# The low parts of the weights made on VectorE instead of GpSimd, from the latent attention's value projection on

## The chip, the cores and the metric

The kernel runs on one core of one Trainium2 chip. The metric is the device time of one execution in microseconds (us). Three runs of the kernel before took 795.70 to 796.46 us, median 796.04. Engines are named as in the profile: PE is TensorE (PEld its weight loads), DVE is VectorE, ACT is ScalarE, POOL is GpSimd, SP is the engine that issues most DMAs. L203 is line 203 of the kernel.

## The reference, cut to what matters

One decoder layer on 512 tokens of width 1024: a convolution branch and a latent attention (MLA) branch, merged by gates, then cross attention to 256 memory tokens, then a squared-ReLU MLP and a final norm. All in float32.

```python
u = rms_norm(h, norm_mix_g)
proj = u @ w_in                     # conv input, c_q, c_kv, k_rope, gate logits
conv_out = conformer_conv(...)      # 31 taps, layer norm, silu, @ w_conv_out
mla_out = mla_attention(...)        # q from w_uq, k and v from w_ukv, 8 heads, @ w_mla_out
merged = gates0 * conv_out + gates1 * mla_out
h = h + merged @ w_out
u = rms_norm(h, norm_xattn_g); mem_n = rms_norm(mem, norm_mem_g)
h = h + memory_cross_attention(u, mem_n, w_xq, w_xkv, w_xo)   # 4 heads of 128
u = rms_norm(h, norm_mlp_g)
h = h + square(relu(u @ w_mlp1)) @ w_mlp2
y = rms_norm(h, final_norm_g)
```

## The kernel before, in words

Every matrix product is made of three passes over rounded operands (`mm3`, L231 to L240): each operand is split into a high part, the value cast to the matmul's format, and a low part, the value less its high part; the three products high x high, low x high and high x low are added in PSUM (L237, L238, L239). The high part is a cast on ACT, the low part one subtraction on DVE or POOL (`split`, L201 to L203; `split_scaled` at L206 and L207 is the same with a factor).

Activations are split once, on ACT and DVE. Weights arrive in raw chunks by DMA from SP (tile `raw`, two buffers, L315) and are split piece by piece just before their use by `prep` (L324): a piece is mostly 128x1024, its high part `wh` and low part `wl` have three buffers each. Which engine makes `wl` is held in a variable, `w_eng[0]`: DVE for the second convolution channel tile, POOL from the third on (L638), DVE again from the cross attention's output projection on (L1147).

A small pipe (`Pipe`) issues the split of the next piece before the matmuls of the piece in hand. PE runs in the order in which the program is written; the order on the other engines is set by a scheduler that goes by estimates of its own, so the place of an instruction on DVE or ACT can differ from its place in the program. Each engine then works through its queue strictly in that order.

The stretch that matters here runs from the value projection to the end of the cross attention's scores. In program order:

- heads: k and v (`k_pair` and the loop that fills `vh`, `vl`), q per head (`q_head`, product with the rotary table into `qtmp` at L763, then split into `q`), `scores` (row maximum `m` at L794, exp on ACT, scaling of `p` at L800), `transp` (transposes of `p` on PE at L810, split into `pt`), `pv` (split into `oh`, `ol`). The convolution's output projection `conv_out` lies between (`gates` at L828). In every odd step of the loop a piece of `uq` (128x768) and one of `co` (128x1024) are split.
- output projection of the attention and merge: `evac_mla` takes each of 8 columns from PSUM times its gate (`mt`, L916), adds the convolution's part (L917) and splits the sum into `mgh` on ACT and `mgl` on DVE.
- `out_unit`: 8 units of 24 matmuls over all 8 merged columns, then `Norm.add` (residual `ht` at L976, its split `hgl` at L207, sum of squares at L983). Memory tokens are normalised meanwhile (`mem_norm`, with `mh` on ACT and `ml` on DVE).
- memory keys `xk_unit` (`xkt`, `xkl`), and beside it the inverse root of the norm (`rsqrt`, L245 to L250, tiny DVE instructions in a chain), whose result PE broadcasts by four transposes (L271).
- cross attention: queries `xq_unit` (`xt`, `xql`), `xscores`, `xtransp`, values `xv_unit`, `xpv`.

The MLP behind it has POOL issue DMAs only.

Of the kernel before, what the change touches and what calls it, by code (L numbers as in the profile page):

```python
# [168 lines left out]
def _body(tc, a):  # L169
# [3 lines left out]
    dve = nc.vector  # L173
# [27 lines left out]
    def split(hi, lo, src, eng=None):  # L201
        act.copy(hi, src)  # L202
        (eng or dve).tensor_tensor(lo, src, hi.bitcast(F32), op=ALU.subtract)  # L203
# [94 lines left out]
    def chunk_hbm(i):  # L298
        n = stream[i][3] * len(stream[i][4])
        return a["weights"][offs[i]:offs[i] + P * n].rearrange("(p n) -> p n", p=P)  # L300

    def raw(*key):
        ci = ch[key]
        while issued[0] < n_ring and issued[0] < ci + RAW_BUFS:
            i = issued[0]
            _, _, _, kt, cols = stream[i]
            n = kt * len(cols)
            t = wp.tile([P, 2048], F32, tag="raw", name="raw", bufs=RAW_BUFS)
            src = chunk_hbm(i)
            raws[i] = t[:, :n].rearrange("p (k m) -> p k m", k=kt)  # L310
            if i == 1:
                for sl in (slice(0, 128), slice(128, 256)):
                    dma(out=raws[i][:, :, sl], in_=src.rearrange("p (k m) -> p k m", k=kt)[:, :, sl])
            else:
                dma(out=t[:, :n], in_=src)  # L315
            issued[0] += 1
        return raws[ci]

    def whl(kt, cols):
        hi = wp.tile([P, 1024], F32R, tag="wh", name="wh", bufs=3)  # L320
        lo = wp.tile([P, 1024], F32R, tag="wl", name="wl", bufs=3)
        return tuple(t[:, :kt * cols].rearrange("p (k m) -> p k m", k=kt) for t in (hi, lo))

    def prep(key, k0=0, kt=None, c0=0, cols=128):  # L324

        r = raw(*key)
        kt = r.shape[1] if kt is None else kt
        hi, lo = whl(kt, cols)
        split(hi, lo, r[:, k0:k0 + kt, c0:c0 + cols], w_eng[0])
        return hi, lo  # L330

    w_eng = [dve]
# [233 lines left out]
    def proj_unit(key, c0, evac):  # L566
        def main(hl):
            b = bank()
            mm3(b, [(lhs(hl, k), (uh[:, k, :], ul[:, k, :])) for k in range(KD)])
            evac(b)  # L570
        pipe.unit(lambda: prep(key, c0=c0), main)
# [147 lines left out]
    def evac_gate(b, i):  # L719
        t = wkp.tile([P, S], F32, tag="sg", name="sg")  # L720
        dve.tensor_tensor(t, b, rbx, op=ALU.mult)  # L721
        act.activation(gates[:, i, :], t, AF.Sigmoid)
# [4 lines left out]
    for i in range(16):  # L727
# [2 lines left out]
                c_unit("ckv", j, KVL + ROPE, c_tags, ckv_done)  # L730
        proj_unit(("gate", i // 2), 128 * (i % 2), lambda b, i=i: evac_gate(b, i))
    split(wkk[:, 0], wkk[:, 1], raw("wk"))
    hlv = prep(("wv",), cols=512)
    pipe.flush()
    while not taps[1]:
# [408 lines left out]
                        n2.add(m, bs[m])  # L1144
        pipe.unit(lambda: prep(("xo", m2 // 2), c0=256 * (m2 % 2), cols=256), main)

    w_eng[0] = dve  # L1147
    for m2 in range(4):
        xo_unit(m2)
    pipe.ahead(lambda: prep(("m1", 0)))  # L1150
# [387 lines left out]
```

## Time and profile before

| | us |
|---|---|
| median of three runs | 796.04 |
| the profiled execution | 797.19 |
| its span, first to last instruction | 795.4 |
| PE busy (3594 matmuls) | 761.3 (96%) |
| DVE busy | 535.3 (67%) |
| ACT busy | 400.6 (50%) |
| POOL busy | 169.7 (21%) |
| mean granted clock of TensorE | 0.984 |

Busy time is the time in which at least one instruction of the engine ran; matmuls overlap, so a matmul of 390 ns on 128x512 starts about 227 ns after the one before. Of POOL's busy time 144.6 us are its 65 low parts at L203; of the chain that ended last PE holds 70% and DVE 19%. The granted clock is the share of full speed that TensorE was given: 1.00 is 2.4 GHz, 0.50 is 1.2 GHz.

### The profile page before, as it was taken

Reading aid. Unit: us, or ns where it says so; the run is one execution under the profiler, and the core shown is the slowest. Engines: PE = TensorE matmul, PEld = TensorE weight load, DVE = VectorE, ACT = ScalarE, POOL = GpSimd, SP = SyncE. Lnnn points to the kernel's source line nnn. Section 1 sums busy time; section 2 is a strip of 40 time slices with the busy share of each in tenths; the row PEclk is TensorE's granted clock in tenths of the full one; section 3 lists DMA queues with packets and bytes.
Section 4 is the critical chain, followed back from the end, with each engine's and each line's share of the span. In section 5 each row is a group of like instructions: output and inputs, shape, how many; then the busy total and the mean of one; then the engine's idle time right before and its main releaser. Section 6 shows DMA issues by size and latency. Waiting matters only on the chain.

```text
span 795.4 us, 9520 instructions
## 1 busy us (share of the span) xinstructions
PE 761.3 (96%) x3594; PEld 627.8 (79%) x3594; DVE 535.3 (67%) x812; ACT 400.6 (50%) x681; POOL 169.7 (21%) x103
## 2 busy tenths in 40 slices
PE   8799999999999998998999999999999979999996
PEld 4589788778788886788887888888888858888785
DVE  5798999843888859758686833243333446667995
ACT  7323333469666537343465644444343445655562
POOL 4444336423312215346320000000000000111000
PEclk9899999999999999899999999999999998999998
DMA  8213223222102144124132324425353596999731
GB/s 280 97 40 113 76 84 128 84 90 97 54 0 107 54 157 162 58 102 146 68 105 106 118 108 146 171 82 224 106 188 129 165 283 239 227 236 213 198 106 53
DMA packets 26989, 103.36 MB, mean 130 GB/s; under 512 B 2368, under 2 KB 9920, under 8 KB 17984
## 3 DMA queue, kind: packets, MB, share of 16 engines
q1 hardware_dynamic: 13600, 67.54, 23.8%
q0 software_dynamic: 2304, 16.78, 10.4%
q10 hardware_dynamic: 11040, 18.45, 6.7%
q8 instruction: 28, 0.46, 0.2%
q14 instruction: 17, 0.14, 0.1%
HBM read 94.37 MB, written 8.39 MB: 129 GB/s over the span
## 4 chain that ended last, share of the span: by engine, by line
PE 70%; DVE 19%; DMA 4%; ACT 4%; issue 3%; SPq 0%; DVEq 0%; ACTq 0%
PE mm L239 18%; PE mm L237 18%; PE mm L238 18%; DVE cv L494 6%; PE at L238 4%; PE at L239 4%; PE at L237 4%; DMA a<-weights 2%; DVE q L203 1%; DVE mt L917 1%; DMA x<-weights 1%; DVE rs_t L248 1%; DMA xr<-xT 1%; PE at L810 1%; DVE sg L721 1%
## 5 line engine op out<-in xcount | busy, mean ns | idle before, releaser
L203 POOL TENSOR_TENSOR wl<-raw,wh 128x1024 fp32r<-128x1024 f32 (+4 forms) x65 | 144.6, 2227 | 252.4 <-ACT wh L202 249.3
L202 ACT CAST wh<-raw 128x1024 fp32r<-128x1024 f32 (+4 forms) x103 | 102.6, 998 | 190.0 <-PE mm L238 146.6
L203 DVE TENSOR_TENSOR wl<-raw,wh 128x1024 fp32r<-128x1024 f32 x38 | 46.5, 1224 | 99.6 <-ACT wh L202 99.6
L237 PE MATMUL mm<-hgh,wh 128*128 128x512 f32 x288 | 113.2, 393 | 0.0
L238 PE MATMUL mm<-hgl,wh 128*128 128x512 f32 x288 | 112.2, 390 | 0.0
L239 PE MATMUL mm<-hgh,wl 128*128 128x512 f32 x288 | 112.2, 390 | 0.0
L494 DVE SCALAR_TENSOR_TENSOR cv<-zpad,vec,cv 128x512 f32<-128x512 f32 x116 | 80.2, 752 | 0.1
L1356 POOL DMA_DIRECT2D x<-weights x12 | 10.6, 880 | 293.8 <-DVE wl L203 273.8
L237 PE MATMUL mm<-uh,wh 128*128 128x512 f32 x176 | 70.7, 402 | 2.3 <-DVE sg L721 2.1
L239 PE MATMUL mm<-uh,wl 128*128 128x512 f32 x176 | 69.3, 394 | 0.5 <-DVE wl L203 0.5
L238 PE MATMUL mm<-ul,wh 128*128 128x512 f32 x176 | 69.3, 394 | 0.0
L239 PEld LDWEIGHTS mm<-hgh,wl 128*128 128x128 f32 x288 | 54.1, 188 | 11.4
L237 PEld LDWEIGHTS mm<-hgh,wh 128*128 128x128 f32 x288 | 54.1, 188 | 10.9
L238 PEld LDWEIGHTS mm<-hgl,wh 128*128 128x128 f32 x288 | 54.1, 188 | 10.9
L203 DVE TENSOR_TENSOR wl<-x,wh 128x1024 fp32r<-128x1024 f32 x25 | 30.4, 1223 | 18.9 <-ACT wh L202 18.9
L237 PEld LDWEIGHTS mm<-uh,wh 128*128 128x128 f32 x176 | 33.5, 190 | 10.7 <-issue 4.2
L239 PEld LDWEIGHTS mm<-uh,wl 128*128 128x128 f32 x176 | 33.5, 190 | 8.1 <-DVE wl L203 1.0
L238 PEld LDWEIGHTS mm<-ul,wh 128*128 128x128 f32 x176 | 33.5, 190 | 6.5
L202 ACT CAST wh<-x 128x1024 fp32r<-128x1024 f32 x25 | 26.1, 1048 | 24.4 <-PE at L239 9.7
L238 PE MATMUL at<-wl,hA 128*128 128x512 f32 x96 | 37.6, 392 | 0.6 <-DVE wl L203 0.6
L239 PE MATMUL at<-wh,hB 128*128 128x512 f32 x96 | 37.4, 390 | 0.0
L237 PE MATMUL at<-wh,hA 128*128 128x512 f32 x96 | 37.4, 389 | 0.0
(392 smaller groups left out, 1772.4 us busy)
## 6 DMA issues: line engine op xcount, KB each, us to landing
raw<-weights SPq DMA_DIRECT2D x42, 1024.0 KB, 4.8
x<-weights POOLq DMA_DIRECT2D x12, 1024.0 KB, 11.4
a<-weights SPq DMA_DIRECT2D x5, 1024.0 KB, 8.3
x<-weights SPq DMA_DIRECT2D x4, 1024.0 KB, 5.9
raw<-weights SPq DMA_DIRECT2D x4, 768.0 KB, 4.3
xr<-xT SPq DMA_DIRECT2D x8, 256.0 KB, 6.0
raw<-weights SPq DMA_DIRECT2D x4, 512.0 KB, 5.0
ht<-xT ACTq DMA_DIRECT2D x1, 2048.0 KB, 9.4
```

The source lines that it names most:

```text
L202: act.copy(hi, src)
L203: (eng or dve).tensor_tensor(lo, src, hi.bitcast(F32), op=ALU.subtract)
L237: pe.matmul(out, wh, ah, start=first and i == 0, stop=False, **kw)
L238: pe.matmul(out, wh, al, start=False, stop=False, **kw)
L239: pe.matmul(out, wl, ah, start=False, stop=last and i == n - 1, **kw)
L248: dve.scalar_tensor_tensor(t, dst, -0.5, dst, op0=ALU.mult, op1=ALU.mult)
L494: dve.scalar_tensor_tensor(run if w < CW - 1 else acc[:, c, :], zs, wcol, run, op0=ALU.mult, op1=ALU.add)
L721: dve.tensor_tensor(t, b, rbx, op=ALU.mult)
L810: pe.transpose(b[:, (t - k) * P:(t - k + 1) * P], ptok[h, t][:, k * P:(k + 1) * P], ident)
L917: dve.tensor_tensor(t, t, gates[:, m, :], op=ALU.add)
L1356: gps.dma_start(out=t, in_=hbm(what, c), accum_op=ALU.add, max_dma_last_dim=8192)
```

## The change

`w_eng[0] = dve` moves up: it stood ahead of the cross attention's output projection (`xo_unit`) and now stands ahead of the split of `wv`, the value projection of the latent attention. 33 low parts change engine: 29 of 128x1024 and 4 of 128x768. Lines behind the new place have numbers higher by 2 (by 1 behind the old place).

```diff
@@ -730,6 +730,8 @@
                 c_unit("ckv", j, KVL + ROPE, c_tags, ckv_done)
         proj_unit(("gate", i // 2), 128 * (i % 2), lambda b, i=i: evac_gate(b, i))
     split(wkk[:, 0], wkk[:, 1], raw("wk"))
+
+    w_eng[0] = dve
     hlv = prep(("wv",), cols=512)
     pipe.flush()
     while not taps[1]:
@@ -1144,7 +1146,6 @@
                         n2.add(m, bs[m])
         pipe.unit(lambda: prep(("xo", m2 // 2), c0=256 * (m2 % 2), cols=256), main)
 
-    w_eng[0] = dve
     for m2 in range(4):
         xo_unit(m2)
     pipe.ahead(lambda: prep(("m1", 0)))
```

The order on PE and SP stays as it was. On DVE the scheduler puts the low parts between the other instructions, and some of these change places. Three places follow.

DVE in the output projection, merged columns 6 and 7 and what follows, before:

```order
L916 TENSOR_TENSOR mt_2964<-mm,gates 128x512
L916 TENSOR_TENSOR mt_2982<-mm,gates 128x512
L917 TENSOR_TENSOR mt_2964<-mt_2964,gates 128x512
L917 TENSOR_TENSOR mt_2982<-mt_2982,gates 128x512
L246 TENSOR_SCALAR rm<-rs_i 128x2
L207 SCALAR_TENSOR_TENSOR ml<-mr,vec,mh 128x256
L203 TENSOR_TENSOR mgl<-mt_2964,mgh 128x512
L203 TENSOR_TENSOR mgl<-mt_2982,mgh 128x512
```

And DVE at the same place now:

```order
L918 TENSOR_TENSOR mt_2964<-mm,gates 128x512
L918 TENSOR_TENSOR mt_2982<-mm,gates 128x512
L919 TENSOR_TENSOR mt_2964<-mt_2964,gates 128x512
L919 TENSOR_TENSOR mt_2982<-mt_2982,gates 128x512
L203 TENSOR_TENSOR wl<-raw,wh 128x1024
L203 TENSOR_TENSOR mgl<-mt_2964,mgh 128x512
L203 TENSOR_TENSOR mgl<-mt_2982,mgh 128x512
L203 TENSOR_TENSOR wl<-raw,wh 128x1024
L978 TENSOR_TENSOR ht<-ht,mm 128x512
```

One low part of the weights stands ahead of the last two `mgl`, one behind them; the memory's small instructions have moved behind. The pairs of columns 2, 3 and 4, 5 have one low part each ahead of their `mgl` in the same way.

DVE in an odd step of the heads, from the scaling of `p` to the first `pt` (the transposed probabilities' low part), before:

```order
L799 RECIPROCAL rl<-l 128x1
L800 TENSOR_SCALAR p<-p,rl 128x512
L763 TENSOR_TENSOR qtmp<-mm,tq 128x512
L203 TENSOR_TENSOR q<-qtmp,q 128x512
L203 TENSOR_TENSOR ol<-mm,oh 64x512
L203 TENSOR_TENSOR pt_1990<-at,pt_1990 128x512
```

And DVE at the same place now:

```order
L765 TENSOR_TENSOR qtmp<-mm,tq 128x512
L801 RECIPROCAL rl<-l 128x1
L802 TENSOR_SCALAR p<-p,rl 128x512
L203 TENSOR_TENSOR wl<-raw,wh 128x1024
L203 TENSOR_TENSOR q<-qtmp,q 128x512
L203 TENSOR_TENSOR ol<-mm,oh 64x512
L203 TENSOR_TENSOR pt_1990<-at,pt_1990 128x512
```

A low part of 128x1024 stands ahead of `q`, and `qtmp` ahead of the last scaling. In the first two odd steps another low part, 128x768, stands ahead of the four row maxima.

DVE at the inverse root of the norm ahead of the cross attention, from its first pass on, before:

```order
L248 SCALAR_TENSOR_TENSOR rs_t<-rr 128x4
L958 TENSOR_TENSOR xkt<-mm,rbm 128x256
L249 TENSOR_TENSOR rs_t<-rs_t,rv 128x4
L250 SCALAR_TENSOR_TENSOR rr<-rs_t,rr 128x4
L248 SCALAR_TENSOR_TENSOR rs_t<-rr 128x4
L249 TENSOR_TENSOR rs_t<-rs_t,rv 128x4
L250 SCALAR_TENSOR_TENSOR rr<-rs_t,rr 128x4
L248 SCALAR_TENSOR_TENSOR rs_t<-rr 128x4
L203 TENSOR_TENSOR xkl<-xkt,xkh 128x256
L249 TENSOR_TENSOR rs_t<-rs_t,rv 128x4
L250 SCALAR_TENSOR_TENSOR rr<-rs_t,rr 128x4
```

And DVE at the same place now, from the second pass on:

```order
L248 SCALAR_TENSOR_TENSOR rs_t<-rr 128x4
L203 TENSOR_TENSOR wl<-raw,wh 128x1024
L249 TENSOR_TENSOR rs_t<-rs_t,rv 128x4
L203 TENSOR_TENSOR xkl<-xkt,xkh 128x256
L250 SCALAR_TENSOR_TENSOR rr<-rs_t,rr 128x4
L248 SCALAR_TENSOR_TENSOR rs_t<-rr 128x4
L249 TENSOR_TENSOR rs_t<-rs_t,rv 128x4
L960 TENSOR_TENSOR xkt<-mm,rbm 128x256
L250 SCALAR_TENSOR_TENSOR rr<-rs_t,rr 128x4
```

One low part stands inside the chain, and one `xkt` more.

## Rows read from the trace of the kernel before

**Rows 1.** A stretch: length, busy us of PE, PEld, DVE, ACT, POOL, clock, DMA share, GB/s.

```profile
180.50:424.00 243.50, 233.82 (x1214) 194.35 (x1214) 183.85 (x320) 138.67 (x280) 78.56 (x33) 0.99 0.27 95
```

**Rows 2.** Waits of PE, 180 to 430 us: total, times, longest.

```profile
PE mm L237 <- ACT mgh L202: 3.1, 1, 3.1
PE at L271 <- DVE rr L250: 2.3, 1, 2.3
PE at L789 <- DVE pt L203: 1.5, 3, 0.5
PE at L792 <- DVE q L203: 1.5, 1, 1.5
PE mm L238 <- DVE mgl L203: 0.7, 2, 0.5
PE at L1100 <- DVE xpt L203: 0.5, 1, 0.5
```

**Rows 3.** Groups by form: busy us, mean ns, idle before; low parts on both engines.

```profile
L203 POOL TENSOR_TENSOR wl<-raw,wh 128x1024 fp32r<-128x1024 f32 x49 | 119.3, 2437 | 185.0 <-ACT wh L202 181.9 <-PE at L810 3.1
...
L203 DVE TENSOR_TENSOR wl<-raw,wh 128x1024 fp32r<-128x1024 f32 x38 | 46.5, 1224 | 99.6 <-ACT wh L202 99.6
```

**Rows 4.** One tile's instructions, xql: duration ns min/median/max, first and last start.

```profile
L203 DVE TENSOR_TENSOR xql<-xt,xqh x4: 2459/2470/2486, 383.5 to 402.7; 128x512 fp32r<-128x512 f32 x4
```

**Rows 5.** Time order, DVE and POOL, output projection: start us, us (start to end).

```profile
297.87 1.29 DVE L917 TENSOR_TENSOR mt<-mt,gates 128x512 f32<-128x512 f32 x2
...
301.65 4.96 DVE L917 TENSOR_TENSOR mt<-mt,gates 128x512 f32<-128x512 f32 x2
...
309.10 2.75 DVE L917 TENSOR_TENSOR mt<-mt,gates 128x512 f32<-128x512 f32 x2
...
300.84 5.22 POOL L203 TENSOR_TENSOR wl<-raw,wh 128x1024 fp32r<-128x1024 f32 x2 [20.12 <-ACT wh L202]
```

**Rows 6.** Time order, PE, first unit of the output projection.

```profile
309.30 0.40 PE L237 MATMUL mm<-mgh,wh 128*128 128x512 f32 x1
...
312.10 0.40 PE L237 MATMUL mm<-mgh,wh 128*128 128x512 f32 x1
...
322.93 0.41 PE L239 MATMUL mm<-mgh,wl 128*128 128x512 f32 x1
```

**Rows 7.** Stretches of the output projection and of the cross queries, with granted clock.

```profile
317.47:322.50 5.03, 4.80 (x11) 3.42 (x11) 3.97 (x11) 2.35 (x4) 0.72 (x1) 0.50 0.00 0
...
360.00:385.00 25.00, 22.72 (x152) 20.61 (x151) 17.62 (x26) 10.17 (x14) 14.51 (x6) 1.00 0.36 127
```

**Rows 8.** Time order, DVE, inverse root ahead of the cross attention.

```profile
372.06 2.25 DVE L250 SCALAR_TENSOR_TENSOR rr<-rs_t,rr 128x4 f32<-128x4 f32 x1
...
374.55 0.16 DVE L249 TENSOR_TENSOR rs_t<-rs_t,rv 128x4 f32<-128x4 f32 x1
374.75 2.34 DVE L250 SCALAR_TENSOR_TENSOR rr<-rs_t,rr 128x4 f32<-128x4 f32 x1
```

**Rows 9.** Time order, DVE, an odd step of the heads.

```profile
221.12 0.49 DVE L800 TENSOR_SCALAR p<-p,rl 128x512 f32<-128x512 f32 x1
...
223.15 2.47 DVE L203 TENSOR_TENSOR q<-qtmp,q 128x512 fp32r<-128x512 f32 x1 [0.95 <-ACT q L202]
```

**Rows 10.** Time order, PE: first scores, an odd step of the heads, the broadcast.

```profile
203.89 0.33 PE L792 MATMUL at<-k,q 128*128 128x128 f32 x1 [1.47 <-DVE q L203]
...
222.31 1.28 PE L810 MATMUL at<-kon,p 128*128 128x128 f32 x10
...
226.87 0.33 PE L789 MATMUL at<-k,q 128*128 128x128 f32 x1 [0.51 <-DVE pt L203]
...
377.94 0.65 PE L271 MATMUL at<-kon,rr 128*128 128x128 f32 x4 [2.28 <-DVE rr L250]
```

**Rows 11.** Time order, ACT: casts of the weights ahead of two of the places.

```profile
199.77 1.06 ACT L202 CAST wh<-raw 128x1024 fp32r<-128x1024 f32 x1
...
299.71 2.00 ACT L202 CAST wh<-raw 128x1024 fp32r<-128x1024 f32 x2
```

## The prediction

> **What bounds the kernel now.** The changed instructions all lie between 180 and 424 us, so the first view is the table by stretches: in these 243.5 us PE is busy 233.8, DVE 183.9 and POOL 78.6 [rows 1]. PE is the bound, and only its 9.7 us of idle time, with what follows from it, can be won; DVE is next. The second view, who waited for whom on PE in this stretch, splits the idle time into six releasers, 9.6 us together [rows 2]. None is POOL: all are ACT or DVE. So why should taking work from POOL matter? The third view, groups by form, has one 128x1024 low part at 2437 ns on POOL and 1224 ns on DVE [rows 3]. The fourth, one tile's instructions, has DVE's 128x512 low part of the cross queries (xql) at 2470 ns median [rows 4], while two DVE additions of the same size take 1.29 us together while POOL is idle, which it is for 20 us until 300.84 [rows 5]. In the time order such stretched instructions start while a POOL low part runs: the next two pairs of additions take 4.96 and 2.75 us. I read this as a hold: DVE stands until POOL's instruction is over, at some 1.8 us each (2.47 less 0.65).
>
> **What the change moves.** 33 low parts go from POOL to DVE: 29 of 128x1024 and 4 of 128x768. DVE gets 29 x 1.22 + 4 x 0.92 (three quarters of 1.22) = 39 us; POOL has no arithmetic left in the stretch. Were each of the 33 to hold one DVE instruction now, DVE would get back 33 x 1.8 = 59 us; bounds for DVE's own work are thus -20 and +39 us. What counts is only where PE waits, place by place. PE, SP and the DMA order are the same in both; a raw buffer can come free up to 1 us later or earlier, which I cost at nothing since the casts of the next weights on ACT wait mostly for PE. If that cover is gone, a late cast costs what it is late.
>
> Place 1, output projection. PE starts its first unit at 309.30 and goes on at 0.233 us a matmul (twelve to 312.10) [rows 6]. In before it waits 0.5 us, then 3.07 us for the seventh merged column, and after that the granted clock is 0.50, the 1.2 GHz level, over 317.47 to 322.50 [rows 7]; the thirtieth matmul starts at 322.93. Without any wait it would start at 309.30 + 29 x 0.233 = 316.06, so 6.9 us are lost. Now DVE in the new order, with 0.6 us from start to start for every free 128x512 instruction and 1.22 for a low part: the two additions that start at 301.65 end at 302.9 instead of 306.5 [rows 5]; low part (its high part is cast by 301.7 [rows 11]) to 304.1; two mgl to 305.35; two products to 306.6; two additions to 307.8; low part to 309.0, 0.8 us before PE wants it; two mgl to 310.4 (five casts of the memory stand ahead of their high halves on ACT, which I estimate costs nothing, since DVE is at the low part meanwhile); two products to 311.65; two additions to 312.9; low part to 314.1; the last two mgl at 314.75 and 315.35. PE wants the first of these with its twentieth matmul, 309.30 + 19 x 0.233 = 313.73, and waits 1.05 us. The wait of 2.28 us elsewhere in the stretch [rows 2] was followed by no slow matmuls (granted clock 1.00 over 360 to 385 us [rows 7]), so I let the clock stay at 2.4 GHz. Gain 6.9 - 1.05 = 5.8. Bounds: 6.9 if DVE is 1 us earlier, 0.5 if the wait again reaches 3 us.
>
> Place 2, norm ahead of the cross attention. Two tiny steps of the inverse root take 2.25 and 2.34 us [rows 8], held like the others; free ones start 0.2 us apart. PE stands 2.28 us for them and goes on at 377.94 [rows 10]. In the new order one low part (1.22) and one more xkl (0.4) lie inside the chain instead: 2 x 2.1 less 1.6 is 2.6, more than the wait. Gain 2.3; if the low part first waits for its cast, 1.1.
>
> Place 3, heads. In each of the three odd steps q's low half starts after its cast and is held (2.47 us from 223.15 [rows 9]), the probabilities' low parts follow, and PE waits 0.5 us for a bank at 226.87 [rows 10]. With the weights' low part (1.22) ahead of q instead of a 1.8 us hold inside it, the bank comes about 1 us sooner. Gain 3 x 0.5 = 1.5. A 0.92 us low part ahead of three row maxima is new there; the last scaled row ends at 221.61 and PE's transposes start at 222.31 [rows 9, 10], so 0.7 us cover it, and a held scaling of p goes too. If that cover is gone it costs 0.2 us a step.
>
> Place 4, first scores. PE goes on at 203.89 after waiting 1.47 us for q's held low half [rows 2, 10]. Now a low part, cast from 199.77 [rows 11] to 200.83, runs on DVE to 202.05 ahead of q's product; product 202.7, cast 203.3, low half 203.95. A wait on the queue takes the hold's place: gain 0. Bounds -1.2 and +1.4.
>
> Place 5, cross attention: 0.5 us for the transposed probabilities [rows 2]; xql ends 0.6 us sooner per head, so gain 0.5 (bounds 0 and 0.5).
>
> For small new waits at places with less than 1 us of cover I take 0.5 off. Sum: 5.8 + 2.3 + 1.5 + 0 + 0.5 - 0.5 = 9.6 us. The profiled execution took 797.19 us with a span of 795.4, 1.15 above the median of 796.04, so the sum gives 787.6 for such an execution and 786.4 for the median.
>
> One rule speaks against the change. The Trainium skill (Perfetto Trace Analysis, Optimizing Scalar/DVE Operations) says that work may be offloaded from a saturated DVE, even to GPSIMD, but that this may not help, as the two share an SBUF port. By its first half this change, made the other way round, would cost time; by its second half it would not. The stretched rows above agree with the second half; the price of the first is the third rival's.
>
> **Rivals.** First, the clock falls all the same at place 1. It needs DVE's chain 2 us later than I worked out, say by ACT's casts of the memory ahead of the merged columns. Then place 1 gives 0.5 and the sum is 4.3: 791.7. For it: DVE is nearly full there, and my chain has eleven steps with no idle time. Against: the two held pairs that go are worth 3.6 and 1.5 us by themselves.
>
> Second, nothing measurable: at every place the low part takes what the hold took, as at place 4. Then only place 2's remainder of 1.1 is left, set against small new waits: 795.5. Against it: a low part is 0.6 us shorter than a hold, and two holds go in place 1 before any low part is added.
>
> Third, slower: DVE's queue becomes the bound among the heads. With no holds given back DVE would have 183.9 + 39 = 223 us of work in 243.5. Nine low parts come between 200 and 296 us (seven of 1.22, two of 0.92): 10.4 us, all on the path of scores, row maxima, scaling and transposes if the stretched rows are slow for a cause other than POOL. Less place 2's 1.1 and place 5's 0.5 that is 8.8 slower, 804.8. It decides from where the last scaled row comes later than the 0.7 us of cover. Against it: free and stretched instructions of one form differ only by POOL's running.
>
> **Chances.** Forecast 0.70, with its own range 783.8 (5.8 becomes 6.9, place 4 gives 1.4) to 789; clock falls 0.15; no change 0.07; slower 0.08. Range for 8 in 10: 783.8 to 792, which takes in the clock rival. About 0.2% (1.6 us) is what a measurement of this kernel can tell from no change. Faster 0.85, within 0.2% 0.07, slower 0.08.
>
> **What would show it.** In the changed profile: no POOL arithmetic after 182 us; DVE's xql near 0.7 us, the additions of place 1 near 0.65 and the small steps of place 2 near 0.16; PE's wait in the first output unit near 1 us with granted clock 1.00 behind it; no wait of PE at the broadcast of place 2; the three waits for a bank gone; at the first scores a wait of 1.3 us for q, now behind a low part. The forecast is wrong if these instructions stay long, if the slow matmuls are still there, or if PE's idle time between 180 and 424 us stays over 6 us.

## The result, and the profile after

The changed kernel takes 785.12 us (median of four runs, 783.22 to 785.32); the kernel before took 796.25 beside it. The ratio is 0.9846, 95% interval 0.9823 to 0.9868. By the medians that is 11.1 us faster, by the ratio 12.3, where 9.6 were forecast. The profiled execution took 785.28 us, with a span of 783.5 (before 795.4).

The table by stretches of the kernel after answers [rows 1, 7]. Columns: stretch, its length, busy us of PE, PEld, DVE, ACT, POOL, granted clock, DMA share, GB/s.

```profile
180.50:424.00 243.50, 241.46 (x1265) 202.57 (x1265) 181.20 (x360) 143.84 (x288) 0.00 (x0) 1.00 0.27 95
308.00:324.00 16.00, 15.73 (x68) 12.39 (x67) 16.00 (x35) 8.06 (x13) 0.00 (x0) 1.00 0.31 101
```

PE's idle time in the stretch fell from 9.7 to 2.0 us, and the 1.2 GHz level of the output projection is gone. DVE works slightly less than before (181.2 against 183.9), although it makes 33 low parts more, and gets through more of the program in this time: over the same 1214 matmuls (181.65 to 413.50 us in the trace after) it is busy 175.4 us, 8.4 less than before.

PE's waits from 175 to 425 us (total, times, longest), beside [rows 2]:

```profile
PE at L791 <- ACT q L202: 1.1, 1, 1.1
PE mm L237 <- DVE k L203: 0.4, 1, 0.4
PE mm L238 <- DVE mgl L203: 0.3, 1, 0.3
PE at L794 <- DVE q L203: 0.2, 1, 0.2
```

The waits for mgh, for the inverse root rr, for a bank (pt) and for xpt no longer stand in the list. The wait for k is new.

The low part of the cross queries, with its duration in ns (minimum, median, maximum), beside [rows 4], and DVE in time order in the output projection (start, us from start to end), beside [rows 5]:

```profile
L203 DVE TENSOR_TENSOR xql<-xt,xqh x4: 683/684/685, 374.3 to 393.9; 128x512 fp32r<-128x512 f32 x4
```

```profile
300.66 1.28 DVE L919 TENSOR_TENSOR mt<-mt,gates 128x512 f32<-128x512 f32 x2
301.86 1.22 DVE L203 TENSOR_TENSOR wl<-raw,wh 128x1024 fp32r<-128x1024 f32 x1
...
305.40 1.28 DVE L919 TENSOR_TENSOR mt<-mt,gates 128x512 f32<-128x512 f32 x2
...
312.48 1.28 DVE L203 TENSOR_TENSOR mgl<-mt,mgh 128x512 fp32r<-128x512 f32 x2
```

2470 ns became 684, and the pairs of additions that took 4.96 and 2.75 us take 1.28, with a low part of 1.22 in the queue behind them.

PE at the same place, beside [rows 6], and at the broadcast, beside [rows 10]:

```profile
308.34 0.40 PE L237 MATMUL mm<-mgh,wh 128*128 128x512 f32 x1
...
312.55 0.40 PE L237 MATMUL mm<-mgh,wh 128*128 128x512 f32 x1
313.21 0.50 PE L238 MATMUL mm<-mgl,wh 128*128 128x512 f32 x1 [0.27 <-DVE mgl L203]
...
315.65 0.40 PE L239 MATMUL mm<-mgh,wl 128*128 128x512 f32 x1
...
368.21 0.60 PE L271 MATMUL at<-kon,rr 128*128 128x128 f32 x4
```

From the first to the thirtieth matmul are 7.31 us instead of 13.63; the broadcast follows the matmul before it with no wait. Its chain on DVE, beside [rows 8]:

```profile
364.25 0.16 DVE L250 SCALAR_TENSOR_TENSOR rr<-rs_t,rr 128x4 f32<-128x4 f32 x1
...
364.55 1.22 DVE L203 TENSOR_TENSOR wl<-raw,wh 128x1024 fp32r<-128x1024 f32 x1
...
366.10 0.15 DVE L250 SCALAR_TENSOR_TENSOR rr<-rs_t,rr 128x4 f32<-128x4 f32 x1
```

The two held steps are 0.16 and 0.15 us, and one low part stands in the chain, as the order said.

### The profile page after: what moved, and what is told of

The parts are those of the page before. It is cut to its first block, busy times and chain, and to the rows that moved or that the text cites. A ratio compares the mean times of both kernels' runs of the same rounds, so it can differ in the third digit from the quotient of the medians.

```text
span 783.5 us, 9480 instructions
## 1 busy us (share of the span) xinstructions
PE 757.7 (97%) x3594; PEld 626.3 (80%) x3594; DVE 526.9 (67%) x845; ACT 400.3 (51%) x681; POOL 91.2 (12%) x70
## 3 DMA queue, kind: packets, MB, share of 16 engines
q0 software_dynamic: 2304, 16.78, 10.5%
## 4 chain that ended last, share of the span: by engine, by line
PE 79%; DVE 13%; DMA 3%; ACT 2%; issue 2%; SPq 0%; DVEq 0%; ACTq 0%
PE mm L239 20%; PE mm L237 20%; PE mm L238 20%; DVE cv L494 6%; PE at L238 4%; PE at L239 4%; PE at L237 4%; DMA a<-weights 2%; PE at L812 1%; PE at L793 1%; DVE wl L203 1%; DMA xr<-xT 1%; DVE rs_t L248 1%; DVE sg L721 1%; PE at L794 1%
## 5 line engine op out<-in xcount | busy, mean ns | idle before, releaser
L203 DVE TENSOR_TENSOR wl<-raw,wh 128x1024 fp32r<-128x1024 f32 (+1 forms) x71 | 85.7, 1207 | 105.7 <-ACT wh L202 105.5
L203 POOL TENSOR_TENSOR wl<-raw,wh 128x1024 fp32r<-128x1024 f32 (+4 forms) x32 | 66.1, 2066 | 96.7 <-ACT wh L202 96.7
L1357 POOL DMA_DIRECT2D x<-weights x12 | 10.5, 879 | 516.1 <-DVE wl L203 496.1
```

The costliest lines, as they stand in the source:

```text
L1357: gps.dma_start(out=t, in_=hbm(what, c), accum_op=ALU.add, max_dma_last_dim=8192)
```

## The experiments

The theory: DVE's instructions were long because POOL's subtraction of the weights' low parts ran beside them. Its rivals: the low parts only came earlier or later; anything long on POOL would do the same; one place carries the whole gain. The kernel before, run beside experiments 1 to 4, took 796.97 us (median), beside 5 to 8 797.24, and beside 9 and 10 798.27.

### 1 to 3: one part of the change at a time

The low parts go to DVE among the heads only (experiment 1), from the output projection to the memory norm only (experiment 2), in the cross attention only (experiment 3). Each diff is against the kernel before; line 1147 stays.

```diff
 # 1: heads
+    w_eng[0] = dve
     hlv = prep(("wv",), cols=512)
...
+    w_eng[0] = gps
     pipe.unit(lambda: None, mla_out_first)
```

```diff
 # 2: output projection
+    w_eng[0] = dve
     pipe.unit(lambda: None, mla_out_first)
...
+    w_eng[0] = gps
     for m in range(XH):
```

```diff
 # 3: cross attention
+    w_eng[0] = dve
     for m in range(XH):
```

> Only the 11 low parts of the value projection, queries, convolution output and first MLA output pieces go to DVE; the other 22 stay on POOL. Hold theory (DVE instructions with two SBUF inputs stand until a POOL low part ends): the three waits of PE for a bank among the heads (0.5 us each) go, the first scores still wait about 1.3 us, PE's wait of 3.1 us in the output projection with the slow matmuls behind it and the 2.3 us at the broadcast stay: 1 to 2.5 us faster than before. Rival (what helps is that low parts of the weights are ready 1.2 us sooner): PE waited for none of them, so nothing among the heads: within 0.5 us of before.

> Only the 10 low parts from the last two MLA output pieces to the last output-projection piece go to DVE. Hold theory: the eight additions of the merge take 0.68 us each instead of up to 2.9, PE's wait shrinks from 3.1 to about 0.3 us, the matmuls of 1.2 GHz behind it are gone, the 2.3 us at the broadcast stay: 6.3 us faster than before (5.5 to 7). Rival (DVE queue order: the low parts only put the memory's small instructions behind): about 1 us faster, since the additions stay long.

> Only the 12 low parts of memory keys, cross queries and values go to DVE. Hold theory: PE's 2.3 us at the broadcast and 0.5 us at the transposed probabilities go, the merge's 3.1 us wait with slow matmuls stays: 3.2 us faster than before (2.2 to 3.7). Together with the two runs beside it the three parts should add up to the whole change's 11.1 us, within 1.5 us. Rival: the parts don't add up, because a place gains only where the one ahead of it was also relieved.

Measured: 794.31 us, ratio 0.9962 (0.9948 to 0.9976); 790.31 us, 0.9914 (0.9897 to 0.9932); 793.62 us, 0.9958 (0.9942 to 0.9975). One less the ratio, times 797 us, gives gains of 3.0, 6.9 and 3.3 us, 13.2 together, against 12.3 for the whole change by its ratio: the parts add up within their intervals, and the output projection is worth half. Against the 11.1 us that I had named the sum is 2.1 too high, more than the 1.5 I allowed, and experiment 1 gained more than its range of 1 to 2.5 us. PE's three longest waits from 175 to 425 us, first of experiment 1, then of 2, then of 3:

```profile
PE mm L237 <- ACT mgh L202: 3.1, 1, 3.1
PE at L271 <- DVE rr L250: 2.3, 1, 2.3
PE at L790 <- ACT q L202: 1.1, 1, 1.1
```

```profile
PE at L271 <- DVE rr L250: 2.2, 1, 2.2
PE at L789 <- DVE pt L203: 1.5, 3, 0.5
PE at L792 <- DVE q L203: 1.5, 1, 1.5
```

```profile
PE mm L237 <- ACT mgh L202: 3.1, 1, 3.1
PE at L789 <- DVE pt L203: 1.5, 3, 0.5
PE at L792 <- DVE q L203: 1.5, 1, 1.5
```

Each part takes away the waits of its own places and leaves the others as they were. In experiment 1 a wait of 1.1 us for ACT's q stands in the place of q's held low half, as in the kernel after.

### 4 and 5: what on POOL holds DVE

Experiment 4 is the change, and POOL repeats a subtraction of the same size (high part less itself, into a tile that nobody reads) after each of the 33 pieces.

```diff
         split(hi, lo, r[:, k0:k0 + kt, c0:c0 + cols], w_eng[0])
+        if twin[0]:
+            d = wp.tile([P, 1024], F32, tag="twin", name="twin", bufs=1)
+            h = hi.bitcast(F32).rearrange("p k m -> p (k m)")
+            gps.tensor_tensor(d[:, :kt * cols], h, h, op=ALU.subtract)
```

> The change, with POOL doing the same number of subtractions of the same sizes again, on the high part alone, into a tile that nobody reads. The low parts are made by DVE as in the change. Hold theory: DVE's xql, q and the merge's additions are long again (up to 2.5 us), and DVE has the low parts on top: slower than before, 797 to 806 us. Rival (sooner low parts are what helped): the time of the change, 784 to 787 us, and DVE's instructions short.

Measured: 804.02 us, ratio 1.0083 (1.0061 to 1.0105). The low parts are still made by DVE, and the whole gain is gone. POOL and DVE in time order:

```profile
306.82 4.20 POOL L333 TENSOR_TENSOR twin<-wh 128x1024 f32<-128x1024 f32 x2 [19.63 <-ACT wh L202]
...
307.57 3.99 DVE L926 TENSOR_TENSOR mt<-mt,gates 128x512 f32<-128x512 f32 x2
```

The pair of additions that takes 1.28 us by itself ends 0.54 us after POOL's two subtractions do. PE waits 5.0 us for the inverse root, 3.4 us for banks and 2.4 us for a low part of the weights in this kernel, and the granted clock is 0.50 from 312.61 to 316.02 us, as the wait for the low part ends, and from 384.29 to 391.11, as the one for the inverse root ends. The 19 us against the change are thus waits and slow matmuls together. One sign came out weaker than expected: only one of the four xql is long (2.39 us, the others 0.68).

In experiment 5 POOL copies one column and then fills the unread tile twice in place of the subtraction.

```diff
+            gps.tensor_copy(d[:, :1], hi.bitcast(F32)[:, 0, :1])
+            gps.memset(d, 0.0)
+            gps.memset(d, 1.0)
```

> The change, and POOL fills an unread tile of 128x1024 twice after each of the 33 prepared weight tiles (one column is copied from the high parts, then two fills that read nothing). Theory A (what held DVE was POOL's subtraction, which reads two tiles, and not that POOL is busy): 784 to 788 us, xql<-xt,xqh 684 ns, q<-qtmp,q 680 to 695 ns, PE's waits in 175:425 about 2 us. Rival B (any long POOL instruction holds DVE's subtraction): xql near 2460 ns, PE's waits for DVE in 175:425 over 8 us, 797 to 805 us as in the run with the repeated subtractions. In between (a hold that ends after each fill): q or mt adds from 900 to 1700 ns, 789 to 794 us.

Measured: 784.43 us, ratio 0.9838 (0.9819 to 0.9857), as the change. Its stretch, then DVE and POOL in time order:

```profile
180.50:424.00 243.50, 241.42 (x1266) 202.56 (x1265) 183.28 (x362) 142.99 (x287) 87.29 (x99) 1.00 0.27 95
```

```profile
300.98 1.22 DVE L203 TENSOR_TENSOR wl<-raw,wh 128x1024 fp32r<-128x1024 f32 x1
...
304.51 1.29 DVE L927 TENSOR_TENSOR mt<-mt,gates 128x512 f32<-128x512 f32 x2
```

```profile
301.29 0.95 POOL L332 COPY twin<-wh 128x1 f32<-128x1 f32 x1
...
304.57 0.96 POOL L333 MEMSET twin<- 128x1024 f32 x1
```

POOL is busy 87.3 us (63.0 of them the fills, 24.2 the copies) where [rows 1] has 78.6, and DVE's additions at 304.51 take 1.29 us through a fill. So POOL's being busy is not what holds DVE. The subtraction reads two operands in SBUF (in experiment 4 the same tile twice) and the fill reads none; that this is the difference that counts I take from the two runs, though another kind of reading instruction was not tried. The copy, which does read, shows the hold the other way: it starts inside DVE's subtraction and ends 0.04 us after it, 0.95 us long, where others close by take 0.18; over the 33 copies the median is 0.90.

The Trainium skill (SBUF — State Buffer, Who interferes with whom) has it that a DVE instruction with two SBUF inputs contends with a GpSimd instruction that reads SBUF and not with one that only writes it. Experiments 4 and 5 agree, with 804.0 and 784.4 us.

### 6 to 8: the change begun earlier, and the change again

Experiment 6 has DVE make the last four gate pieces' low parts too; experiment 7 is the change once more; experiment 8 has DVE make every low part from L638 on.

```diff
 # 6, in the loop over the gate pieces
+        if i >= 12:
+            w_eng[0] = dve
         proj_unit(("gate", i // 2), 128 * (i % 2), lambda b, i=i: evac_gate(b, i))
```

```diff
 # 8
-        w_eng[0] = dve if c == 1 else gps
+        w_eng[0] = dve
```

> The change begun earlier: also the last four gate pieces' low parts on DVE (POOL keeps 28). Theory: it removes the one held instruction left behind 170 us, the rr product at 173.15 (2.39 us), which lies in the chain of the key latent's scale; PE has no listed wait of over 0.5 us there, so 783 to 786 us, no difference from the change within 0.3%. Rival: DVE, busy 118 of the 135 us up to 180, is late for its own evacuations: PE waits `mm L237 <- DVE sg L721` grow by 2 us or more, 787 to 790 us.

> The change again, beside the others on the same chip. 783.5 to 787 us. If the later start of the key projection (191.84 against 190.69) is a matter of the execution, it starts at 190.6 to 190.9 here as in three of the four experiments; if it belongs to the change, at 191.8. The wait of PE for ACT's s among the last matmuls lies between 4.1 and 5.6 us in any execution.

> The change extended to every low part that POOL still makes from the choice of line 638 on (two gated pieces, the latents' down projections, all gate pieces). Theory: DVE takes some 20 more subtractions of 1.2 us, 24 us, where it is busy 118 of 135 us, and its conv steps move later; held instructions there go, which give back about as much. PE waits 2.5 us in 45:180 after the change, so no gain over 2 us: 784 to 790 us. Rival (the hold costs PE among the gates as much as behind them): 780 to 783 us. Rival (DVE becomes the bound there): over 792 us, with PE waiting for sg or for the conv steps before 190.

Measured: 784.69 us, ratio 0.9840 (0.9818 to 0.9861); 785.56 us, 0.9848 (0.9824 to 0.9871); 786.66 us, 0.9866 (0.9847 to 0.9886). Experiment 6 makes no difference; the held step that I named for it belongs to the inverse root of the convolution's layer norm (lnr), and it did go (0.16 us). In 7 the key projection starts at 191.30, between the two values that I had set against each other; over nine traces (before, after, experiments 1 to 7) it lies between 190.7 and 192.2, with and without the change.

What moves it is TensorE's clock early in the kernel. In all nine PE waits 4.9 to 5.0 us for a broadcast at 35.4 to 36.1 us, and about that time a stretch at the 1.2 GHz level begins, of varying place and length. The seven us from the broadcast on, in the trace of before and in that of after (the third number from the end is the granted clock):

```profile
35.41:42.41 7.00, 7.00 (x24) 5.79 (x25) 2.98 (x6) 4.06 (x5) 0.00 (x0) 0.70 0.00 0
35.64:42.64 7.00, 7.00 (x21) 5.66 (x22) 2.72 (x6) 3.81 (x5) 0.00 (x0) 0.56 0.00 0
```

By that, PE loses 30% of seven us before and 44% after, 1.0 us more, and the broadcast comes 0.23 us later; together that makes up the 1.15 us. Less what the slow stretch takes (half its time from the broadcast on), the time from the broadcast to the key projection is 153.15 to 153.26 us in all nine traces. So the later start belongs to the execution and not to the change.

In 8 there is a gain and a loss. DVE and PE in time order:

```profile
59.37 4.05 DVE L494 SCALAR_TENSOR_TENSOR cv<-zpad,vec,cv 128x512 f32<-128x512 f32 x6
...
63.92 0.95 DVE L203 TENSOR_TENSOR wl<-raw,wh 128x768 fp32r<-128x768 f32 x1
```

```profile
64.93 0.69 PE L238 MATMUL at<-wl,uh 128*128 128x384 f32 x1 [5.78 <-DVE wl L203]
```

The low part of the query latent's first piece stands behind a run of convolution steps in DVE's queue, six of them after PE has begun to wait, and PE stands 5.78 us for it. Then it runs at the 1.2 GHz level until 70.64 (granted clock 0.50), which is another 2.9 us. The wait at the broadcast, on the other hand, fell from 4.9 to 2.0 us.

### 9 and 10: the version that these point to

Experiment 9 is experiment 8 with the four low parts of the query latent left on POOL. Experiment 10 is the change with the four low parts of the last two gated pieces on DVE as well, and nothing else.

```diff
 # 9 and 10
-        w_eng[0] = dve if c == 1 else gps
+        w_eng[0] = dve
...
+    w_eng[0] = gps
     for i in range(4):
         c_unit("cq", i, QL, c_tags, cq_done)
+    w_eng[0] = dve          # 9 only
```

> As the extension to every low part, but the four low parts of the query latent's down projection stay on POOL. In that run PE waited 5.8 us at 64.93 for the first of them, which stood behind six conv steps on DVE. Theory: that wait goes and the 2.9 us gained at the broadcast near 30 us (2.0 us of issue against 4.9) stays: 780 to 783 us, below the change by 0.3 to 0.6%. Rival (what the wait took comes back as another: the conv steps held by POOL's four instructions, or PE's faster arrival at the next weights): 784 to 787 us. Rival (slower than the change: DVE late for the gates' sg): over 787 us.

> The change, and only the low parts of the last two gated pieces on DVE as well; the latents' down projections and the gates stay on POOL. Theory: what the extension gained lies near 30 us alone (the wait at the broadcast), so 781 to 784 us, the same within 0.2% as the run with the four latent low parts on POOL and the gates on DVE. Rival (the gates' low parts carry part of it): 784 to 786 us here and 781 there.

Measured: 781.70 us, ratio 0.9794 (0.9775 to 0.9813), and 780.78 us, 0.9781 (0.9767 to 0.9795). Both beat the change (0.9848, 0.9824 to 0.9871); the second, with the simpler edit, is the fastest kernel here, some 5 us below the change and 0.2 below the range that I gave it. The two do not differ beyond their intervals, so the gates' low parts carry nothing net. In the waits they do show: PE's 2.1 us for sg between 40 and 190 us are there in 10 and gone in 9, where waits of 2.6 us for a low part (wl) and for the latents' columns (cql, ckl) have come instead. Where the gain comes from, first in the kernel after, then in experiment 10:

```profile
24.96 4.82 POOL L203 TENSOR_TENSOR wl<-raw,wh 128x1024 fp32r<-128x1024 f32 x2
...
25.06 4.88 DVE L444 TENSOR_SCALAR ang<-kon,posf 128x16 f32<-128x16 f32 x4
...
35.64 1.09 PE L271 MATMUL at<-kon,rx 128*128 128x128 f32 x4 [4.89 <-issue]
```

```profile
26.44 0.65 DVE L444 TENSOR_SCALAR ang<-kon,posf 128x16 f32<-128x16 f32 x4
...
32.95 0.62 PE L271 MATMUL at<-kon,rx 128*128 128x128 f32 x4 [2.00 <-issue]
```

Four tiny instructions ahead of the first norm's inverse root were held for 4.88 us by two low parts on POOL; without them they take 0.65, and PE goes on 2.7 us earlier. The key projection then starts at 187.47. Of the 4.4 us against the kernel after 2.7 are thus shown. Another 1.3 are the clock: over the seven us from the broadcast on it is 0.76 in experiment 10 and 0.56 in the kernel after (in 9 it is 1.00). Whether the shorter wait causes the higher clock is not shown, since the slow stretch differs between executions too. The last 0.4 are not split.

## Why the forecast was right, point by point

I set the start of each stage in the trace after against the trace before; a step's gain is what the difference changes by over its place.

**The hold.** As predicted: xql 684 ns, the additions 1.28 us a pair, the small steps 0.16, no arithmetic on POOL. Experiments 4 and 5 show the cause, and that a POOL instruction that only writes does not hold, which I had not asked. I had bounded DVE's own work by -20 and +39 us; it came to -8.4 over the same matmuls.

**Place 1, output projection.** Forecast 5.8, measured 6.3 (13.63 less 7.31). The remaining wait was to be 1.05; the trace has 0.27. The chain from the additions at the start to the last pair of mgl took 11.82 us where I had summed 12.45: I had added durations from start to end, though instructions of DVE start 0.05 to 0.1 us before the one ahead of them ends. The clock stayed at 2.4 GHz, as I had let it.

**Place 2, inverse root.** Forecast 2.3, measured 2.45: the broadcast comes 9.73 us earlier, the thirtieth matmul ahead of it 7.28.

**Place 3, heads.** Forecast 1.5, measured 2.5 (from the first transposes to the output projection 97.11 us before, 94.64 after). This is the term that was mis-sized most. The three waits of 0.5 us did go, but a wait costs more than its listed time. PE at the first of them, beside [rows 10], before and then after, from the matmul ahead of the scores to the first score of the second block:

```profile
225.97 0.39 PE L239 MATMUL mm<-yh,wl 128*128 128x512 f32 x1
...
227.33 0.38 PE L789 MATMUL at<-k,q 128*128 128x256 f32 x1
```

```profile
227.48 0.39 PE L239 MATMUL mm<-yh,wl 128*128 128x512 f32 x1
...
228.06 0.33 PE L791 MATMUL at<-k,q 128*128 128x256 f32 x1
```

1.36 us became 0.58, so 0.78 are regained with 0.51 listed. The other two places give 0.80 and 0.77, so the three are worth 2.35 of the 2.5.

**Place 4, first scores.** Forecast 0, measured -0.35 (190.69 to 212.19 before, 191.84 to 213.70 after). PE and DVE there, beside [rows 10]:

```profile
197.88 0.47 PE L237 MATMUL mm<-wh,ckh 128*128 128x512 f32 x1 [0.45 <-DVE k L203]
...
204.66 0.33 PE L791 MATMUL at<-k,q 128*128 128x128 f32 x1 [1.05 <-ACT q L202]
```

```profile
194.15 0.96 DVE L203 TENSOR_TENSOR wl<-raw,wh 128x768 fp32r<-128x768 f32 x1 [0.56 <-ACT wh L202]
195.03 0.68 DVE L203 TENSOR_TENSOR k<-mm,k 64x512 fp32r<-64x512 f32 x1
...
202.13 1.23 DVE L203 TENSOR_TENSOR wl<-raw,wh 128x1024 fp32r<-128x1024 f32 x1 [0.39 <-ACT wh L202]
203.27 0.68 DVE L765 TENSOR_TENSOR qtmp<-mm,tq 128x512 f32<-128x512 f32 x1
```

The wait on the queue did take the hold's place: 1.05 us here and 0.2 more for q's low half, where I had 1.3. What I had missed is a low part of uq ahead of the first k, for which PE waits 0.45 us.

**Place 5, cross attention.** Forecast 0.5, measured 0.8: the first transpose behind the wait for xpt comes 10.5 us earlier, the broadcast 9.7.

**Small new waits.** Forecast -0.5; apart from the one at k there are none.

These sum to 6.3 + 2.45 + 2.5 - 0.35 + 0.8 = 11.7. Two things come on top that I did not foresee: the key projection started 1.15 us later, by the clock, as above, and one wait of PE in the MLP, for ACT's s, was shorter. It was 5.6 in the trace of before, 4.3 and 4.7 in two executions of the change, and 3.7 to 5.6 over the traces of the experiments, a wider span than the 4.1 to 5.6 that I had put on record ahead of experiment 7; I see no order in it, and why it moves stays open. 11.7 - 1.15 + 1.3 = 11.85 of the 11.9 by which the span fell. That these two nearly cancel is luck.

**The rivals.** The clock did not fall again at place 1 (1.00 over 308 to 324). That nothing would be measurable is refuted. The third, that DVE's queue would be the bound and the stretched rows slow for another cause, is refuted by experiment 4, where the low parts are on DVE and POOL's subtractions are put back. Its picture of a queue that is too full does occur, where I had not looked for it: at 64.93 us in experiment 8. The Trainium skill (Perfetto Trace Analysis, Optimizing Scalar/DVE Operations) says that taking work off DVE for GPSIMD need not help; the runs agree, since there it cost what the change gives back, 1.5%.

## What to carry to other kernels

The time order of two engines shows such a hold: the same instruction is short where the other engine is idle, and ends with the other's instruction where it is not. Before giving elementwise work to a third engine, look at what it will read beside, and move it only to stretches whose DVE instructions are not stretched by it; a held tiny step in a serial chain (2.3 us here) can cost more than the piece of work that was moved (1.2 us). When adding up a queue use the distance from start to start; a listed wait of PE that went gave back some 0.17 to 0.27 us more than its length here.

## What the runs showed of the hardware beyond that

Not every DVE instruction is held by POOL's subtractions. The convolution steps of the kernel after, whose running sum lies in a PSUM bank, beside POOL:

```profile
117.70 11.93 DVE L494 SCALAR_TENSOR_TENSOR cv<-zpad,vec,cv 128x512 f32<-128x512 f32 x18
```

```profile
120.04 1.44 POOL L203 TENSOR_TENSOR wl<-raw,wh 128x576 fp32r<-128x576 f32 x1 [1.99 <-ACT wh L202]
123.61 2.40 POOL L203 TENSOR_TENSOR wl<-raw,wh 128x1024 fp32r<-128x1024 f32 x1 [2.13 <-ACT wh L202]
126.81 2.42 POOL L203 TENSOR_TENSOR wl<-raw,wh 128x1024 fp32r<-128x1024 f32 x1 [0.81 <-ACT wh L202]
```

18 steps run at 0.66 us each straight through three subtractions. So the long part of DVE's work among the gates runs free. The small part does not: a step of a latent's inverse root, beside POOL's subtraction from 140.71 to 143.10 us,

```profile
141.14 1.98 DVE L248 SCALAR_TENSOR_TENSOR rs_t<-rr 128x4 f32<-128x4 f32 x1
```

is held, and the sg for which PE waits 0.90 us at 146.06 stands behind it in DVE's queue. This is one of the two waits for sg that experiments 8 and 9 take away; 9 has other waits in their place, and 6, whose pieces come later, leaves them as they are. The tiny steps at L444 have one tensor input in SBUF and were held all the same, 4.88 us for four. The Trainium skill (SBUF — State Buffer, Who interferes with whom) lists a DVE instruction with at most one SBUF input as free of contention, unless it runs in a 2-port mode, which it says tensor_scalar, the operation of L444, can enter; no run here shows the mode of L444.
